# Two delta heads' keys and queries: written by GpSimd straight into the delta rule's tiles, instead of through DRAM

## The chip, the cores and the metric

One core of one Trainium2 chip. The core has five engines that run side by side, each with its own queue of instructions in a fixed order: TensorE (PE in the profile; its weight loads are PEld), VectorE (DVE), ScalarE (ACT), GpSimd (POOL) and SyncE (SP). SP computes nothing here; it issues nearly all the transfers (DMAs) between DRAM and the on-chip memory SBUF. PE writes only into PSUM, the accumulation memory, of which this kernel uses eight banks of 128 x 512 float32. The metric is device microseconds (us) for one execution, the median of several runs.

## The reference

One decoder layer on 1024 tokens of width 1024. A normalised input goes through one projection of 4104 columns. Eight heads of stick-breaking attention and four heads of a gated delta rule work on parts of it, and both results go through an output projection, with a residual and a final norm. For the change only the delta rule's entrance matters:

```python
qkv = jax.nn.silu(causal_depthwise_conv(jnp.concatenate([g_q, g_k, g_v], axis=-1), gdn_conv_w[layer]))
gq, gk, gv = jnp.split(qkv, 3, axis=-1)
gq = l2norm(to_heads(gq, GDN_HEADS, GDN_HEAD_DIM)).astype(x.dtype)
gk = l2norm(to_heads(gk, GDN_HEADS, GDN_HEAD_DIM)).astype(x.dtype)
...
o_gdn = gated_delta_chunked(gq, gk, gv, decay, beta)
```

Here `silu(y)` is `y * sigmoid(y)`: the last product of the projection of a delta head. `gated_delta_chunked` walks the tokens in chunks; each chunk's output needs the state that the chunk before has left.

## The kernel before

The kernel is written with several generators ("streams"): `projections` (the filler, with weight 100 at the end of the file), the delta rule in five streams (`delta_pre`, `delta_load`, `delta_substitute`, `delta_solve`, `delta_scan`), `attention` and `attention_values`, and the output stage. `interleave` takes a step of the most urgent stream that is ready and, where none is, a piece of the filler. "Ready" is judged by `Model`, a planner in the Python code that runs while the program is built: it holds an estimated cost for each instruction and a clock for each engine. The order in which the planner starts instructions on VectorE, ScalarE, GpSimd and SyncE, and in which steps are taken for TensorE, becomes the fixed order of each engine's queue. So an instruction that the planner thinks ready earlier moves in every queue, and so does much of what comes after it. On the chip an engine works strictly down its queue; one whose next instruction is not ready waits.

The filler goes through `ORDER`: projections of the delta heads 0 to 3 (`G0` to `G3`, three kinds each, in the order keys 1, queries 0, values 2), of attention values (`v1`), attention keys (`k0` to `k3`) and gates (`z`). Each kind is two halves of 512 tokens, and each half 24 products of 128x512 (three per 128 rows of the input, since float32 operands are split into a high and a low part). Over the kernel that makes 1152 such products, in the profile `pp<-xh,weh` and the like. The output of one half is handled by `g_evac`: ScalarE copies it out (`pre`), VectorE runs the four taps of the convolution into `ac`, ScalarE takes the sigmoid (over the no longer needed `pre`), and GpSimd multiplies the two (`ac<-ac,pre`).

A unit of the delta rule is half of a head (h, g), 512 tokens in four chunks. Its keys and queries stand in one tile `kq` (128 partitions x 4 chunks x 2 kinds x 128 tokens; `kqf` in the profile, `kwf` where it is read by a transpose), for which SBUF has four fixed slots (`Fixed`, tag "kq"). Before the first delta head these slots hold four rows of the raw input. `delta_load` fetches `kq` with two DMAs from a DRAM copy, `g_s`, that `g_evac` has stored. For the first two heads (`TURNED` = 2) nothing else of the keys is stored, and `gdn_pre` turns keys and queries with eight PE transposes of 128x128; heads 2 and 3 take turned copies from DRAM (`gt_s`). `gdn_pre` then forms the products of each chunk's keys with keys and queries (`pz<-kqf`, 128x256, four a unit), and later multiplies the queries by a decay in place (`kqf<-kqf,cb` on GpSimd). `gdn_chain` is the sequential part; at its end the slot is free for the unit four further on. The values of a delta head (`vt`) come from DRAM in all cases.

Attention values are split and stored (`v_s`) early, and each attention head loads its own into one tile, `v2a`, once the head before has read it.

Nearly all DMAs stand in SP's queue, in the planner's order. All instructions recorded by the planner carry line 363 in the profile (`ins = f(*args, **kw).ins`), so the rows are told apart by their tiles.

Of the kernel before, what the change touches and what calls it, by code (L numbers as in the profile page):

```python
# [10 lines left out]
F32 = mybir.dt.float32  # L11
# [3 lines left out]
ALU = mybir.AluOpType  # L15
AX = mybir.AxisListType

P = 128
# [13 lines left out]
TURNED = 2  # L32
# [4 lines left out]
OUT_WEIGHTS, DELTA, WEIGHTS, BANK, WINDOW, OUTPUT, RESULT, DECAYS = -1, 0, 2, 5, 10, 12, 20, 25  # L37
# [441 lines left out]
def block(tc, xT_d, x_d, n1_d, wE_d, wQ_d, wC_d, conv_d, alog_d, dtb_d, mixw_d, wo_d, fnw_d, out_d):  # L479
    nc = tc.nc  # L480
    ck = Model({"V": nc.vector, "A": nc.scalar, "G": nc.gpsimd, "P": nc.tensor, "S": nc.sync})
    V, A, G, TE, S = ck.V, ck.A, ck.G, ck.P, ck.S

    with ExitStack() as top:
# [7 lines left out]
        fx = Fixed(ck, nc, {**{f"sg{w}": (2048 * (w + 1), 1) for w in range(4)}, "o2": (1024, 1), "kq": (4096, 4), "ak": (4096, 4)})  # L492
# [23 lines left out]
        half = cst.tile([P, SBH], F32, name="half")  # L516
# [18 lines left out]
        g_s = dr.tile([GH, 3, P, T], F32, name="g_s")  # L535
# [21 lines left out]
        def turned(tp, parts):  # L557
            ck.hold(tp)
            for u, a in enumerate(parts):
                if a.dtype == F32R:  # L560
                    TE.transpose(tp[:, u * P:(u + 1) * P].bitcast(F32R), a, idr)
                else:
                    TE.transpose(tp[:, u * P:(u + 1) * P], a, ident)
            ck.free(tp)
            yield from ()
# [58 lines left out]
        for tag, bufs in (("kh", 1), ("kl", 1), ("q2", 1), ("v2a", 1), ("sg2", 1), ("cc", 2), ("cc", 2), ("sg3", 1)):  # L624
            if tag[0] == "s":
                chl.append(fx.tile([P, 2, 520], F32R, "chl", tag))
            else:
                t = at_.tile([P, 1040 + (48 if tag == "kl" else 0)], F32R, tag=tag, bufs=bufs, name="chl")
# [15 lines left out]
        raw, loads = [], {}  # L644
# [78 lines left out]
        def first(f, *args, bank=BANK, **kw):  # L723
            ck.prio, prio = bank, ck.prio
            f(*args, **kw)
            ck.prio = prio
# [49 lines left out]
        flags = {}  # L776
# [88 lines left out]
        def z_evac(i):  # L865
# [9 lines left out]

            return evac

        def g_evac(h, kind):
            wv = conv[:, 4 * kind + h, :]
            last = []  # L880

            def evac(pt, half):
                pre = gd.tile([P, 515], F32, tag="pre", bufs=2, name="pre")
                if half == 0:
                    V.memset(pre[:, 0:3], 0.0)
                else:
                    A.activation(pre[:, 0:3], last[0][:, 512:515], AF.Copy)
                last.append(pre)
                first(A.activation, pre[:, 3:515], pt, AF.Copy)
                ac = pr.tile([P, 512], F32, tag="kt", bufs=2, name="ac")  # L890

                first(A.activation, pt, pre[:, 0:512], AF.Copy, scale=wv[:, 0:1])
                for i in range(1, 4):
                    first(V.scalar_tensor_tensor, ac if i == 3 else pt, pre[:, i:i + 512], wv[:, i:i + 1], pt, ALU.mult, ALU.add)
                sg = pre[:, 0:512]
                first(A.activation, sg, ac, AF.Sigmoid)
                first(G.tensor_tensor, ac, ac, sg, ALU.mult)
                ts = slice(half * 512, half * 512 + 512)
                if h < TURNED:
                    return S.dma_start(g_s[h, kind, :, ts], ac)  # L900
                done = [S.dma_start(g_s[h, kind, :, ts], ac)] if kind < 2 else []
                first(V.transpose, sg, ac)
                turned = gt_s[h, kind, ts, :].rearrange("(b r) d -> r b d", r=32)
                return done + [S.dma_start(turned[:, :, 32 * a:32 * a + 32], sg[32 * a:32 * a + 32, :].rearrange("r (b c) -> r b c", c=32)) for a in range(4)]

            return evac

        def projections():
# [29 lines left out]
            while nxt:  # L938
# [7 lines left out]
                for half in range(2):  # L946
                    hs = slice(half * 512, (half + 1) * 512)
                    wide = name[:2] == "G0" and half
                    yield lambda: ps.room("pz", 4) if wide else ps.room("pp", 2)
                    pt = pz() if wide else pp()  # L950
                    for k in range(NK):
                        n = 8 * half + k
                        if n == 2:
                            nxt = take()
                        if n == 8:
                            split(nxt, 1)
                        if n == 12:
                            split(nxt, 2)
                        h, l = cols.hl[k // 4]
                        mm3(pt, h[:, k % 4, :], l[:, k % 4, :], xh[:, k, hs], xl[:, k, hs], k == 0, k == NK - 1)  # L960
                        if ((k % 4 == 3 if name[0] in 'Gz' else k % 2) or name in ('z0', 'z1', 'z2', 'z3')) and k < NK - 1:
                            yield
                    if half == 0:
                        if name[0] == "G":
                            ev = g_evac(int(name[1]), int(name[2]))
                        else:
                            ev = {"k": k_evac, "z": z_evac}[name[0]](int(name[1]))
                    flags[name if half else name + ".0"] = ev(pt, half)
                    yield
# [21 lines left out]
        def delta_load():  # L991
            yield lambda: "dec" in flags
            for h in range(GH):
                for g in range(2):
                    u = 2 * h + g
                    gst[h, g] = {}
                    half = "" if g else ".0"
                    yield lambda: u < 4 or f"c{u - 4}" in flags
                    if u > 3:
                        yield flags[f"c{u - 4}"]  # L1000
                    kq = fx.tile([P, 4, 2, P], F32, "kq", "kq")
                    ts = slice(512 * g, 512 * g + 512)
                    loads = []
                    for kind in (1, 0):
                        yield lambda: f"G{h}{kind}{half}" in flags
                        loads.append(S.dma_start(kq[:, :, 1 - kind, :], g_s[h, kind, :, ts].rearrange("p (c t) -> p c t", c=4)))
                    ak = fx.tile([P, 2, 4, P], F32, "ak", "ak")
                    kn, at = ak[:, 0], ak[:, 1]
                    nkv = gd.tile([P, 4, P], F32, tag="nkv", bufs=4, name="nkv")
                    gst[h, g].update(kq=kq, kn=kn, nkv=nkv, at=at)  # L1010
                    ck.hold(kq, kn, nkv)
                    turned = lambda kind: gt_s[h, kind, ts, :].rearrange("(c t) d -> t c d", t=P)
                    if h >= TURNED:
                        loads += [S.dma_start(kn, turned(1)), S.dma_start(nkv, turned(0))]
                    flags[f"l{u}g"] = loads
                    yield lambda: f"G{h}2{half}" in flags and (u == 0 or f"q{u - 1}" in flags)
                    vt = gd.tile([P, 4, P], F32 if h >= TURNED else F32R, tag="vt", name="vt")
                    flags[f"v{u}g"] = S.dma_start(vt, turned(2)) if h >= TURNED else S.dma_start(vt.rearrange("p c t -> p (c t)").bitcast(F32), g_s[h, 2, :, ts])
                    gst[h, g].update(vt=vt)
# [566 lines left out]
        def products_attention():  # L1586
            yield lambda: f"d{NB - 1}" in flags
            for b in range(NB):
# [3 lines left out]
                for got in product(b, 0, parts):  # L1592
# [44 lines left out]
        interleave(ck, lambda: ps.room("pz", 4),  # L1637
                   [Stream(delta_scan(), 0, DELTA), Stream(delta_solve(), 0.5, DELTA + 0.5), Stream(delta_substitute(), 0.6, DELTA + 0.6),
                    pre, Stream(delta_load(), 0.4, DELTA + 0.4), Stream(attention(), 9.995, WINDOW), Stream(attention_values(), 9.99, WINDOW), Stream(out_rows(), 9.1, OUT_WEIGHTS), Stream(out_weights(), 9, OUT_WEIGHTS), Stream(out_weights_attention(), 9.25, OUTPUT + 1), Stream(out_rest(), 9.26, OUTPUT + 1), Stream(enter_x(), 9.31, OUTPUT - 4), Stream(out_norm(0), 9.15, OUTPUT - 1), Stream(out_norm(1), 9.16, OUTPUT - 1), fill,
                    Stream(enter_delta(), 9.3, OUTPUT), Stream(prepare(1), 9.2, OUTPUT), Stream(products_delta(), 101, OUTPUT),  # L1640
                    Stream(enter_attention(), 9.1, OUTPUT - 3), Stream(prepare(0), 9.05, OUTPUT - 2), Stream(products_attention(), 102, OUTPUT - 1.5)])
# [38 lines left out]
```

## Time and profile before

| | us |
|---|---|
| median of 3 runs | 637.29 |
| lowest, highest | 636.22, 638.86 |
| the profiled execution | 639.53 |
| its span, first to last instruction | 637.8 |
| PE busy in it | 624.0 |
| granted PE clock, mean | 0.994 |

A row of the profile's tables of groups reads: line, engine, operation, tile written <- tiles read, shapes, xcount, then busy us and mean ns, then the idle time of the engine just before and what ended it. "SPq" is the time that SP takes to issue a transfer, not the transfer. In a timeline a row begins with its start and its duration in us.

### The profile page before, as it was taken

What the parts mean: (1) busy time and instruction counts of PE and PEld (TensorE: products, weight loads), DVE (VectorE), ACT (ScalarE), POOL (GpSimd) and SP (SyncE); (2) the same over time, 40 slices, a digit from 0 to 9 for tenths busy, and PEclk for the clock granted to TensorE, in tenths of its full rate; (3) what the DMA queues carried; (4) which work ended last, traced back from release to release, by engine and by line L of the source; (5) the groups of instructions that cost most, each with busy time, mean ns of one, the idle gap of its engine ahead of it and who ended that gap; (6) DMA issues with size and microseconds to landing.
All of it is one profiled execution on the core that took longest, in us unless ns stands there. A gap on an engine that the chain in (4) does not pass through costs nothing.

```text
span 637.8 us, 11259 instructions
## 1 busy us (share of the span) xinstructions
PE 624.0 (98%) x3672; PEld 528.7 (83%) x3672; DVE 447.5 (70%) x810; ACT 393.9 (62%) x945; POOL 341.2 (53%) x429
## 2 busy tenths in 40 slices
PE   8999999999999999999999989999999999999995
PEld 7889988988888888788888777888888888888884
DVE  4379973322797798887797696777889774478754
ACT  6665567724786776775785866666777653232553
POOL 0124047728794696881679684386764325245522
PEclk9999999999999999999999999899999999999998
DMA  8958337856557466598668768453652578984322
GB/s 305 342 183 312 124 131 253 303 189 222 159 151 224 131 185 134 141 207 221 167 146 224 185 133 264 121 185 94 180 141 84 151 201 255 311 319 143 116 100 100
DMA packets 165563, 120.21 MB, mean 188 GB/s; under 512 B 96448, under 2 KB 131456, under 8 KB 165504
## 3 DMA queue, kind: packets, MB, share of 16 engines
q1 hardware_dynamic: 165216, 119.29, 62.3%
q8 instruction: 29, 0.48, 0.3%
q14 instruction: 30, 0.25, 0.1%
q10 hardware_dynamic: 288, 0.20, 0.1%
HBM read 80.22 MB, written 39.23 MB: 187 GB/s over the span
## 4 chain that ended last, share of the span: by engine, by line
PE 81%; DMA 6%; ACT 4%; DVE 3%; SPq 2%; issue 2%; POOL 1%; POOLq 0%; DVEq 0%; ACTq 0%
PE pp L363 52%; PE pz L363 21%; PE po L363 6%; PE pc L363 3%; SPq L363 2%; DVE cc L363 1%; DMA v2a<-v_s 1%; DMA kh<-qk_s 1%; DMA xr1f<-xT 1%; DMA o_s<-oe 1%; ACT sgf L363 1%; POOL ac L363 1%; DMA qk_s<-sqh 1%; ACT pz L363 1%; DMA cb<-cum_s 1%
## 5 line engine op out<-in xcount | busy, mean ns | idle before, releaser
L363 PE MATMUL pp<-xh,weh 128*128 128x512 f32 x360 | 146.4, 407 | 0.4 <-DVE ac L363 0.4
L363 PE MATMUL pp<-xh,wel 128*128 128x512 f32 x360 | 141.8, 394 | 0.0
L363 PE MATMUL pp<-xl,weh 128*128 128x512 f32 x360 | 141.3, 392 | 0.0
L363 POOL TENSOR_TENSOR sgf<-sgf,cc 128x128 f32<-128x128 f32 (+3 forms) x64 | 77.5, 1216 | 57.7 <-DVE cc L363 52.5
L363 POOL TENSOR_TENSOR wel<-wer,weh 128x512 fp32r<-128x512 f32 x48 | 62.5, 1305 | 72.0 <-ACT weh L363 71.6
L363 PEld LDWEIGHTS pp<-xh,wel 128*128 128x128 f32 x360 | 68.0, 189 | 15.3
L363 PEld LDWEIGHTS pp<-xh,weh 128*128 128x128 f32 x360 | 68.1, 189 | 12.8 <-DVE ac L363 0.9
L363 PEld LDWEIGHTS pp<-xl,weh 128*128 128x128 f32 x360 | 68.1, 189 | 11.5
L363 DVE TENSOR_TENSOR_SCAN cc<-pz,step 128x384 f32<-128x384 f32 (+2 forms) x64 | 53.4, 844 | 10.6 <-ACT pz L363 9.5
L363 ACT ACTIVATE sgf<-pz,rs 128x384 f32<-128x384 f32 (+3 forms) x96 | 53.5, 593 | 7.6 <-PE pz L363 7.6
L363 DVE TENSOR_TENSOR ahl<-pz,ahl 128x512 fp32r<-128x512 f32 (+1 forms) x80 | 49.5, 630 | 12.0 <-ACT ahl L363 11.3
L363 ACT ACTIVATE ahl<-pz 128x512 fp32r<-128x512 f32 (+1 forms) x80 | 43.2, 559 | 20.6 <-PE pz L363 20.1
L363 ACT ACTIVATE pz<-pz,ns 128x384 f32<-128x384 f32 (+3 forms) x96 | 52.5, 576 | 0.0
L363 PE MATMUL po<-ahl,v2a 128*128 128x512 f32 (+1 forms) x160 | 48.9, 400 | 2.4 <-DMA v2a<-v_s 2.3
L363 PE MATMUL pp<-wo,mmf 128*128 128x512 f32 x192 | 45.5, 396 | 0.0
L363 DVE SCALAR_TENSOR_TENSOR pp<-pre,conv,pp 128x512 f32<-128x512 f32 x42 | 31.4, 747 | 18.2 <-ACT pp L363 17.8
L363 PEld LDWEIGHTS pp<-wo,mmf 128*128 128x128 f32 x192 | 35.8, 188 | 8.4
L363 PE MATMUL pp<-woh,mmf 128*128 128x512 f32 (+2 forms) x136 | 41.9, 385 | 0.0
L363 DVE TENSOR_TENSOR_SCAN cc<-pz,cc,step 128x512 f32<-128x512 f32 (+1 forms) x32 | 38.8, 1211 | 4.1 <-ACT pz L363 3.0
L363 POOL TENSOR_TENSOR mmf<-mgf,mmf 128x512 fp32r<-128x512 f32 x16 | 21.9, 1366 | 37.0 <-ACT mmf L363 23.9
L363 POOL TENSOR_TENSOR ac<-ac,pre 128x512 f32<-128x512 f32 x24 | 31.0, 1293 | 16.3 <-ACT pre L363 10.9
L363 DVE TENSOR_TENSOR xr<-pp,xr 128x512 f32<-128x512 f32 (+2 forms) x33 | 22.2, 672 | 23.0 <-PE pp L363 23.0
(317 smaller groups left out, 1513.9 us busy)
## 6 DMA issues: line engine op xcount, KB each, us to landing
wer<-wE SPq DMA_DIRECT2D x48, 256.0 KB, 3.5
xr<-x SPq DMA_DIRECT2D x16, 512.0 KB, 7.6
g_s<-ac SPq DMA_DIRECT2D x20, 256.0 KB, 2.3
v_s<-v2e SPq DMA_DIRECT2D x16, 256.0 KB, 3.3
kqf<-g_s SPq DMA_DIRECT2D x16, 256.0 KB, 4.0
v2a<-v_s SPq DMA_DIRECT2D x8, 512.0 KB, 5.9
q<-qk_s SPq DMA_DIRECT2D x8, 512.0 KB, 4.5
kh<-qk_s SPq DMA_DIRECT2D x8, 512.0 KB, 3.9
```

The lines of the kernel that those rows point to most:

```text
L363: ins = f(*args, **kw).ins
```

## The change

For the keys and queries of heads 0 and 1, GpSimd's last product goes directly into the unit's `kq` tile, chunk by chunk, instead of over `ac`; the store to `g_s` and the load from it go. The tile is taken from its slot when the first such product is recorded (`operand`), no longer when the load is due. `delta_load` hands on the product itself as the thing to wait for. Values of all heads, and everything of heads 2 and 3, stay as they were.

```diff
+        operands = {}
+
+        def operand(h, g):
+            if (h, g) not in operands:
+                operands[h, g] = fx.tile([P, 4, 2, P], F32, "kq", "kq")
+                ck.hold(operands[h, g])
+            return operands[h, g]
...
                 first(A.activation, sg, ac, AF.Sigmoid)
+                ts = slice(half * 512, half * 512 + 512)
+                if h < TURNED and kind < 2:
+                    kq = operand(h, half)
+                    ck.prio, prio = BANK, ck.prio
+                    r = G.tensor_tensor(kq[:, :, 1 - kind, :], ac.rearrange("p (c t) -> p c t", c=4), sg.rearrange("p (c t) -> p c t", c=4), ALU.mult)
+                    ck.prio = prio
+                    return r
                 first(G.tensor_tensor, ac, ac, sg, ALU.mult)
-                ts = slice(half * 512, half * 512 + 512)
                 if h < TURNED:
                     return S.dma_start(g_s[h, kind, :, ts], ac)
...
-                    kq = fx.tile([P, 4, 2, P], F32, "kq", "kq")
+                    kq = operand(h, g)
                     ts = slice(512 * g, 512 * g + 512)
                     loads = []
                     for kind in (1, 0):
                         yield lambda: f"G{h}{kind}{half}" in flags
-                        loads.append(S.dma_start(kq[:, :, 1 - kind, :], g_s[h, kind, :, ts].rearrange("p (c t) -> p c t", c=4)))
+                        loads.append(flags[f"G{h}{kind}{half}"] if h < TURNED else S.dma_start(kq[:, :, 1 - kind, :], g_s[h, kind, :, ts].rearrange("p (c t) -> p c t", c=4)))
...
-                    ck.hold(kq, kn, nkv)
+                    ck.hold(kn, nkv)
```

On PE, at the end of head 0's projection (the difference of the two orders; `pp` and `pz` are banks, `step` holds the identity matrix for the transposes, `chl` the weights of the attention values):

```order
 L363 MATMUL pp<-xl,weh 128x512
 L363 MATMUL pp<-xh,wel 128x512
+L363 MATMUL pz<-step,kwf_1119 128x128 x8
 L363 MATMUL pp<-xh,weh 128x512
 L363 MATMUL pp<-xl,weh 128x512
@@ -465,4 +466,5 @@
 L363 MATMUL pz<-xl,weh 128x512
 L363 MATMUL pz<-xh,wel 128x512
+L363 MATMUL pz<-kqf_889 128x256 x4
 L363 MATMUL pp<-chl,xh 128x256 x2
 L363 MATMUL pp<-chl,xl 128x256
```

The eight transposes of the first unit now stand after the 12th of the 24 products of the first half of head 0's values, and its four products of keys right behind that projection; both used to stand among the attention values' products further down. On GpSimd the instructions ahead of the first unit's two products are the same as before.

On SP, in the same stretch (`dtf`, `dt`, `cb` and `cum_s` belong to the decays of all heads, `wer` are weights):

```order
-L363 DMA g_s<-ac 128x512 x2
-L363 DMA kqf_1074<-g_s 128x4x128
 L363 DMA cum_s<-cs 32x2x128
-L363 DMA dtf_1009<-cum_s 128x512
-L363 DMA g_s<-ac 128x512
-L363 DMA dtf_1017<-cum_s 128x512
+L363 DMA dtf_1008<-cum_s 128x512
+L363 DMA dtf_1016<-cum_s 128x512
 L363 DMA dt<-cum_s 128x512
```

The stores and loads of keys and queries are gone, and the decay loads stand next to each other. In the whole program SP has 16 transfers fewer, eight `g_s<-ac` and eight `kqf<-g_s`.

Much further on, on SP, ahead of the load of attention head 3's values (`o_s` are attention outputs, `gt_s` turned delta operands, `bd` and `br` belong to the delta rule's inverse). Before:

```order
L363 DMA o_s<-oe 32x8x32 x4
L363 DMA cb<-cum_s 128x512
L363 DMA dt<-dt_s 128x512
L363 DMA wer<-wE 128x512 x2
L363 DMA g_s<-ac 128x512
L363 DMA gt_s<-pre 32x16x32 x4
L363 DMA v2a<-v_s 128x8x128
```

And now:

```order
L363 DMA o_s<-oe 32x8x32 x3
L363 DMA br<-bd 64x1x496 x2
L363 DMA wer<-wE 128x512 x2
L363 DMA o_s<-oe 32x8x32
L363 DMA g_s<-ac 128x512
L363 DMA gt_s<-pre 32x16x32 x4
L363 DMA v2a<-v_s 128x8x128
```

The decay loads `cb` and `dt` of a delta unit no longer stand ahead of this load. Between the last product that reads one attention head's `v2a` and the first that reads the next head's, PE's order had 60 projection products for head 3 and 30 for head 4; it now has 36 and 42. The last head's last such product stands after 1056 of the 1152 projection products before, after 1089 now.

## The prediction, made before the run

> **What bounds the kernel now.** I read the page first, for the busy shares, then the table by stage, then the list of what TensorE (PE) waited for, then the queue of SP, from which nearly every transfer is issued.
>
> ```profile
> span 637.8 us, 11259 instructions
> PE 624.0 (98%) x3672; PEld 528.7 (83%) x3672; DVE 447.5 (70%) x810; ACT 393.9 (62%) x945; POOL 341.2 (53%) x429
> PE 81%; DMA 6%; ACT 4%; DVE 3%; SPq 2%; issue 2%; POOL 1%; POOLq 0%; DVEq 0%; ACTq 0%
> ```
>
> PE is busy for 624.0 of 637.8 us, and 81% of the chain that ended last is PE. So the kernel ends when PE has worked off a list that is fixed at build time; another engine, or a transfer, matters only where PE reaches an instruction too early. About 13.8 us of the span have no PE work. The table by stage (columns: PE, weight loads, DVE, ACT, POOL, then granted clock and DMA) says where:
>
> ```profile
> 0.00:16.00 16.00, 14.20 (x58) 11.70 (x59) 7.26 (x16) 9.74 (x14) 0.98 (x7) 1.00 0.85 306
> ...
> 112.00:128.00 16.00, 15.71 (x129) 15.30 (x128) 5.08 (x14) 12.59 (x41) 11.55 (x16) 1.00 0.88 311
> ...
> 352.00:368.00 16.00, 14.18 (x76) 11.33 (x74) 11.13 (x20) 15.19 (x54) 10.68 (x15) 1.00 0.75 198
> 368.00:384.00 16.00, 15.04 (x76) 12.63 (x77) 15.20 (x25) 9.41 (x19) 12.83 (x11) 1.00 0.60 132
> 384.00:400.00 16.00, 14.50 (x153) 12.05 (x152) 9.65 (x21) 10.26 (x34) 6.90 (x12) 0.96 0.90 267
> 400.00:416.00 16.00, 16.00 (x88) 13.16 (x87) 11.45 (x22) 9.93 (x24) 6.92 (x7) 0.94 0.43 120
> ...
> 624.00:640.00 16.00, 7.21 (x42) 6.25 (x40) 5.42 (x12) 3.99 (x11) 3.99 (x6) 0.82 0.25 99
> ```
>
> The first slice lacks 1.80 us (loading) and the last slice 6.6 of the 13.8 us that belong to the span (the tail after the last product). Neither is touched. Between them PE lacks 13.8 - 1.8 - 6.6 = 5.4 us, of which the three slices from 352 to 400 us hold 1.82 + 0.96 + 1.50 = 4.3. The eight slices from 80 to 208, in which heads 0 and 1 enter the delta rule, add up to 127.71 of 128 us of PE work (below), and all of their 0.29 us lies between 112 and 128. The clock column adds a second loss: (1 - 0.96) and (1 - 0.94) of 16 us make 1.6 us lost to a lower clock between 384 and 416. Which wait ends last there:
>
> ```profile
> PE po L363 <- DMA v2a<-v_s: 2.3, 1, 2.3
> PE po L363 <- DVE step L363: 1.7, 1, 1.7
> PE pz L363 <- ACT wy L363: 1.5, 1, 1.5
> PE pz L363 <- DVE cc L363: 0.6, 2, 0.4
> PE pp L363 <- DVE ac L363: 0.4, 1, 0.4
> PE pz L363 <- ACT nkv L363: 0.3, 1, 0.3
> ```
>
> ```profile
> sum 128.00, PE 127.71 PEld 110.22 DVE 71.48 ACT 82.41 POOL 84.70; mean PE 15.96 PEld 13.78 DVE 8.94 ACT 10.30 POOL 10.59
> ```
>
> Neither the spill `g_s` nor the key and query tile `kq` (called `kqf` in the trace) is in this list. The largest named wait is one load of attention values, `v2a`.
>
> **The change, part by part.** First the product itself.
>
> ```profile
> L363 POOL TENSOR_TENSOR ac<-ac,pre 128x512 f32<-128x512 f32 x24 | 31.0, 1293 | 16.3 <-ACT pre L363 10.9 <-issue 4.5 <-POOL wy L363 0.8
> L363 POOL TENSOR_TENSOR kqf<-kqf,cb 128x512 f32<-128x512 f32 x8 | 10.3, 1287 | 6.6 <-PE pz L363 6.6
> ```
>
> Eight of the 24 products on POOL now write into `kq`, whose rows of 128 lie 256 elements apart. The second row is a product that already reads and writes exactly that layout: 1287 ns against 1293. The eight cost 8 x (1287 - 1293) ns, which is nothing.
>
> Second, the transfers. Eight stores and eight loads of 256 KB go.
>
> ```profile
> g_s<-ac SPq DMA_DIRECT2D x20, 256.0 KB, 2.3
> kqf<-g_s SPq DMA_DIRECT2D x16, 256.0 KB, 4.0
> L363 SPq DMA_DIRECT2D g_s<-ac x20: 319/330/751, 88.7 to 339.8; - x20
> L363 SPq DMA_DIRECT2D kqf<-g_s x16: 371/434/522, 91.2 to 380.6; - x16
> 182.60 0.38 SPq L363 DMA_DIRECT2D kqf<-g_s  x1
> q1 hardware_dynamic: 165216, 119.29, 62.3%
> ```
>
> On SP's queue that is 8 x 0.33 + 8 x 0.43 = 6.1 us of issue time, all of it before 185 us (the last `kqf` load of head 1 goes out at 182.6), and 4.2 of 119.29 MB. For a unit (half a head) the operand is there one store, one issue and one load earlier, 2.3 + 0.4 + 4.0 = 6.7 us. What stood behind those sixteen on SP (the decay loads `dtf`, the weights `wer`, `cb`, `vt`) moves up. On PE it is worth next to nothing now: the delta steps of heads 0 and 1 lie among projection products, and the whole stretch of 80 to 208 us lacks 0.29 us, which the `ACT nkv` row names at 0.3. In the new order the eight transposes and their squares come ahead of the values' projection, so I count that row as gone: **-0.3 us**. If the cover went (a transpose reached before POOL's product was done) PE would wait; the product that it needs ended in time before:
>
> ```profile
> 96.42 1.29 POOL L363 TENSOR_TENSOR ac<-ac,pre 128x512 f32<-128x512 f32 x1 [1.90 <-ACT pre L363]
> 95.62 5.44 PE pp L363 x24
> ```
>
> This is the third product, head 0's queries, first half. It ends at 97.71. The new place of the transposes is after 12 of the 24 products that begin at 95.62, at about 95.62 + 12 x 0.227 = 98.3 (5.44 / 24 = 0.227). Some 0.6 us of margin: the bounds of this wait are 0 and about one POOL instruction, 1.3 us, if another slips in front. I take 0, since the instructions ahead of it on POOL stay the same. Nothing else on PE can be late there but the projection behind it.
>
> Third, **what the new order moves elsewhere**. The planner sees the delta rule ready earlier and lays out everything behind it anew, on all engines. PE's instructions are the same ones, so the sum of the work is unchanged, and only the waits can differ. The one I can follow is `v2a`: each head's load goes out after the head before has read the tile, from an SP queue that is late.
>
> ```profile
> 303.27 1.06 PE L363 MATMUL po<-ahl,v2a 128*128 128x512 f32 x4
> 305.12 0.45 SPq L363 DMA_DIRECT2D cb<-cum_s  x1
> 305.61 1.98 SPq L363 DMA_DIRECT2D dt<-dt_s  x1
> 310.75 1.59 SPq L363 DMA_DIRECT2D wer<-wE  x2
> 314.77 2.04 SPq L363 DMA_DIRECT2D gt_s<-pre  x4
> 316.91 0.48 SPq L363 DMA_DIRECT2D v2a<-v_s  x1
> 324.76 0.59 PE L363 MATMUL po<-ahl,v2a 128*128 128x512 f32 x2
> 350.97 1.06 PE L363 MATMUL po<-ahl,v2a 128*128 128x512 f32 x4
> 361.87 0.38 SPq L363 DMA_DIRECT2D v2a<-v_s  x1
> 361.87 7.05 DMA v2a<-v_s
> 368.96 0.62 PE L363 MATMUL po<-ahl,v2a 128*128 128x512 f32 x2 [2.33 <-DMA v2a<-v_s]
> ```
>
> Head 3: last read over at 304.3, issue at 316.9, 12.6 us late, behind weights and the transposed stores; first use 7.85 us after the issue, so 0.8 us to spare against the 7.05 of the other load. Head 4: read over at 352.0, issue 9.8 us late, and PE waits 2.33. In the new order PE has 36 projection products between the two uses of head 3 where it had 60, and 42 where it had 30 for head 4. At 0.227 us that is 5.4 us less cover for head 3 and 2.7 us more for head 4. With SP as late as before, head 4's 2.3 us vanish and head 3 waits 5.4 - 0.8 = 4.6: together +2.3. With head 3's load early enough, only the -2.3 stays. SP's rows ahead of head 3's load are about as many as before, but `cb` and `dt` (305.12 to 307.6 on SP) are no longer among them; those two were followed by a wait for `wer` that would have hidden their going. So the bounds are -2.3 and +2.3. I take **-1.0**, nearer to the lower end, because the planner puts the first use where it expects the tile to have landed, and in six of seven heads of the trace PE did not wait there.
>
> Sum: 0 - 0.3 - 1.0 = -1.3 us. The profiled execution took 639.53 us (span 637.8, the rest around it), 2.2 above the median of 637.29; it becomes 638.2, and the median **636.0**. A difference of 0.5%, 3.2 us, is about what a measurement of this kernel can tell from no change; so the forecast is "no change that can be told", on the fast side.
>
> The lower clock is a place to weigh a rule. The two rows lost 1.6 us though PE was busy for 14.50 of 16 us and never waited longer than 2.3 us at once. The Trainium skill, "TensorE: Matmul & The Clock Gate", section "Part 1: The HAM clock gate (the "warmup" mystery)", says that the clock falls to half after an idle window of about 3.4 us. By it no fall would be due here; the trace shows one, so the measurement decides.
>
> **The rivals.**
>
> *Middle waits go (faster).* The waits from 352 to 400 us are coincidences of one order, and the new one may not have them: -4.3 - 0.3 gives 632.7. For it: with less on SP, the tightest stretch starts differently. Against: SP is relieved only up to 185 us, a stretch in which PE lacks 0.29 us. With every middle wait and the clock's 1.6 gone the end is -5.4 - 1.6 = -7.0, that is 630.3.
>
> *Head 3's values come late (slower).* Same mechanism as above, other end: 36 products cover too little of 12.6 + 7.05 us, and head 4's wait is not won back since its load again stands behind a row of SP's that waits. +4.6 for head 3 gives 641.9. It decides from an issue more than 12.6 - 4.6 = 8.0 us behind the last read. For it: the attention stream as a whole now stands later against the projections (PE ends its last head's values after 1089 of 1152 products, before after 1056), so cover at the end shrinks as well. Against: the rows ahead of the load are no more than before.
>
> *Nothing reaches PE.* The waits are redone at the same size, 637.3. For it: PE's list is the same, and no wait named `kqf` or `g_s`.
>
> *A second fall of the clock.* A new wait among the many small products of the delta rule's inverse costs another 1.6 us: 636.0 + 1.6 = 637.6. By the skill's window it would take an idle PE of 3.4 us first.
>
> **How the numbers follow.** Forecast 0.42, middle waits gone 0.25, head 3 late 0.21, nothing 0.06, second fall 0.06. Faster by over 0.5% means below 634.1, slower above 640.5. Faster: nearly all of the 0.25 and 0.04 of the forecast's spread, 0.28. Slower: 0.19 of the 0.21 and 0.01 of the clock's, 0.20. The rest, 0.52, is no change. The range takes in both rivals' prices, 632.7 and 641.9, with 1 us beyond the lower one towards its bound of 630.3: 631.5 to 642.0.
>
> **What would show it.** Right: eight products `kqf<-ac` of about 1.29 us on POOL; 12 stores `g_s` and 8 loads `kqf` left; the first transposes of `kq` at about 98 us (not 109.9 as now) with no PE wait for POOL; head 4's wait for `v2a` gone and head 3's below 2 us. Wrong: a POOL product well over 1.3 us, a PE wait on `kqf` near 98 us, head 3 waiting 4 us or more, or a new wait for a transfer in the middle, which would mean that the order's side effects outweigh the transfers that went. An end outside the range would show that the rest of the order, which I did not follow, decides.

## The result, and the profile after

| | before | after |
|---|---|---|
| median | 638.08 us (4 runs) | 647.17 us (4 runs) |
| lowest, highest | 636.22, 640.95 | 646.23, 647.54 |
| ratio, 95% interval | | 1.0149 (1.0123 to 1.0174) |
| profiled execution, its span | 639.53, 637.8 | 647.01, 645.3 |

The changed kernel is slower by 1.5%, 9.1 us, and lies outside the range of 631.5 to 642.0. (The ratios here and below are those of the undisturbed runs, and need not be the quotient of two medians.) The page of the changed kernel, with the lines that were shown of before:

```profile
span 645.3 us, 11215 instructions
PE 626.1 (97%) x3672; PEld 530.1 (82%) x3672; DVE 452.6 (70%) x810; ACT 394.0 (61%) x945; POOL 343.1 (53%) x429
PE 76%; DMA 6%; POOL 5%; DVE 4%; issue 4%; ACT 2%; SPq 2%; POOLq 0%; DVEq 0%; ACTq 0%
```

The span grew by 7.5 us; nearly all of the rest of the 9.1 is that the profiled execution of before lay 1.5 us above its median. PE works off the same 3672 products; its busy time grew by 626.1 - 624.0 = 2.1, and the time without PE work from 13.8 to 645.3 - 626.1 = 19.2, by 5.4. The table by stage (columns as before; the last three are granted clock, DMA share, GB/s) says where:

```profile
256.00:272.00 16.00, 12.44 (x59) 10.32 (x58) 9.40 (x18) 9.27 (x33) 9.46 (x9) 0.89 0.81 195
272.00:288.00 16.00, 14.91 (x74) 12.05 (x73) 14.40 (x27) 13.71 (x34) 13.15 (x19) 1.00 0.60 147
...
352.00:368.00 16.00, 15.65 (x88) 12.98 (x87) 10.99 (x20) 13.12 (x49) 6.09 (x7) 1.00 0.76 185
368.00:384.00 16.00, 13.26 (x48) 10.54 (x49) 9.46 (x15) 6.20 (x17) 12.80 (x16) 0.79 0.95 237
384.00:400.00 16.00, 16.00 (x149) 13.13 (x148) 11.48 (x24) 12.89 (x41) 9.05 (x14) 1.00 0.59 160
...
576.00:592.00 16.00, 14.46 (x70) 11.66 (x70) 12.59 (x18) 3.46 (x5) 6.66 (x4) 1.00 0.29 95
```

Two of these slices as they were before:

```profile
256.00:272.00 16.00, 15.60 (x79) 12.78 (x79) 13.34 (x24) 12.75 (x43) 13.48 (x10) 1.00 0.61 134
...
576.00:592.00 16.00, 16.00 (x78) 12.97 (x77) 12.94 (x20) 4.12 (x9) 6.52 (x5) 1.00 0.40 125
```

In the stretch from 352 to 400 us, PE lacks 0.35 + 2.74 = 3.1 us where it lacked 4.3; its waits of before are gone, and the 2.74 is a new one. Also new are 3.56 + 1.09 us from 256 to 288 and 1.54 from 576 to 592 (before: 0.40 and none). The granted clock is low in two of these slices, 0.89 and 0.79, which by the column makes 1.8 + 3.4 = 5.1 us; before had 0.96 and 0.94 in two later slices, 1.6 us. The list of what PE waited for:

```profile
PE pz L363 <- DVE cc L363: 4.9, 3, 3.6
PE pp L363 <- POOL wel L363: 2.7, 1, 2.7
PE po L363 <- DVE step L363: 1.7, 1, 1.7
PE pp L363 <- ACT mmf L363: 1.5, 1, 1.5
PE pp L363 <- DVE zt L363: 0.5, 1, 0.5
PE pp L363 <- DVE v2e L363: 0.4, 1, 0.4
```

Neither `v2a` nor `nkv` nor `kqf` is in it. The row of `step` (1.7) is the one of before, at the kernel's start; of the others `cc` was at 0.6 before and the rest absent. The first of the new waits, at 260 us, in the timeline of the changed kernel, on SP, DVE and PE (start, us, engine, operation, tile, count, in brackets the idle time before and its end):

```profile
254.44 2.10 SPq L363 DMA_DIRECT2D xs<-xd  x1
256.65 1.00 SPq L363 DMA_DIRECT2D wer<-wE  x2
258.01 1.59 SPq L363 DMA_DIRECT2D gt_s<-pre  x3
257.55 0.65 DVE L363 TENSOR_TENSOR_SCAN cc<-pz,step 128x256 f32<-128x256 f32 x1
262.14 0.06 DVE L363 MEMSET pre<- 128x3 f32 x1 [3.93 <-DMA gt_s<-pre]
262.20 2.07 DVE L363 TENSOR_TENSOR_SCAN cc<-pz,step 128x384 f32<-128x384 f32 x2
263.30 0.43 PE L363 MATMUL pz<-step,stf 128*128 128x128 f32 x3 [3.56 <-DVE cc L363]
```

It is read from the bottom. PE waits for an attention scan `cc`. The scan stands on DVE behind a memset of 0.06 us that clears the head of a convolution tile `pre`; the memset waits 3.93 us until the stores that read this tile have landed. Those stores stand on SP behind `xs<-xd`, which holds SP for 2.10 us. Three queues, each in a fixed order, pass one late row on to an attention step that has nothing to do with it. The second wait, at 375 us, on ACT, POOL and PE:

```profile
368.95 0.67 ACT L363 ACTIVATE weh<-wer 128x512 fp32r<-128x512 f32 x1
369.43 1.55 POOL L363 TENSOR_TENSOR tt<-yx,xb 128x512 f32<-128x512 f32 x1
373.26 1.04 POOL L363 TENSOR_TENSOR norms<-norms,half 128x4 f32<-128x4 f32 x1
374.43 1.46 POOL L363 TENSOR_TENSOR qn<-ss,root 128x4 f32<-128x4 f32 x1
376.65 1.26 POOL L363 TENSOR_TENSOR wel<-wer,weh 128x512 fp32r<-128x512 f32 x1
377.97 0.79 PE L363 MATMUL pp<-xh,wel 128*128 128x512 f32 x1 [2.74 <-POOL wel L363]
```

The weights' high part is ready at 369.6; their low part `wel`, which needs only that, stands on POOL behind the delta rule's inverse and its norms, and starts 7 us later.

### The profile page after: what moved, and what is told of

Read it like the earlier page. It is cut to its first block, busy times and chain, and to the rows that moved or that the text cites. A ratio compares the mean times of both kernels' runs of the same rounds, so it can differ in the third digit from the quotient of the medians.

```text
span 645.3 us, 11215 instructions
## 1 busy us (share of the span) xinstructions
PE 626.1 (97%) x3672; PEld 530.1 (82%) x3672; DVE 452.6 (70%) x810; ACT 394.0 (61%) x945; POOL 343.1 (53%) x429
## 4 chain that ended last, share of the span: by engine, by line
PE 76%; DMA 6%; POOL 5%; DVE 4%; issue 4%; ACT 2%; SPq 2%; POOLq 0%; DVEq 0%; ACTq 0%
PE pp L363 44%; PE pz L363 22%; PE po L363 6%; PE pc L363 3%; SPq L363 2%; DVE cc L363 1%; POOL mmf L363 1%; DMA gt_s<-pre 1%; DMA worf<-wo 1%; DMA dtf<-cum_s 1%; POOL tt L363 1%; DMA og_s<-akf 1%; POOL oss L363 1%; DVE pp L363 1%; DMA bothf<-o_s 1%
## 5 line engine op out<-in xcount | busy, mean ns | idle before, releaser
L363 PEld LDWEIGHTS pz<-step,stf 128*128 128x128 f32 x288 | 30.7, 141 | 8.3 <-issue 3.7
L363 PE MATMUL pz<-step,stf 128*128 128x128 f32 x288 | 34.0, 244 | 3.6 <-DVE cc L363 3.6
```

## The experiments

The theory to start from: the direct write itself costs nothing; the order that the planner lays out for it does, through rows like the two above. The rival: the write, or the lack of the transfers, costs by itself.

### The cross: the write without its order, and the order without the write

The first kernel has the direct write in the order of before. The planner still records the old product, stores and loads, and rows without an instruction are left out at the end:

```diff
+        def ghost(out, src):
+            op = ck.record("S", None, [out], [src], cost("S", "dma_start", (out, src), {}), None)
+            op.port = False
+            return op
...
+                    ins = nc.gpsimd.tensor_tensor(kq[:, :, 1 - kind, :], ac.rearrange("p (c t) -> p c t", c=4), sg.rearrange("p (c t) -> p c t", c=4), ALU.mult).ins
...
+                    op = ck.record("G", ins, [ac], [ac, sg], cost("G", "tensor_tensor", (ac, ac, sg, ALU.mult), {}), None)
...
+                    return ghost(g_s[h, kind, :, ts], ac)
...
-                        loads.append(S.dma_start(kq[:, :, 1 - kind, :], ...))
+                        loads.append((ghost if h < TURNED else S.dma_start)(kq[:, :, 1 - kind, :], g_s[h, kind, :, ts].rearrange("p (c t) -> p c t", c=4)))
...
+                    ck.hold(kq, kn, nkv)
...
         for ops in ck.order.values():
+            ops = [o for o in ops if o.ins is not None]
```

> The eight products of heads 0 and 1 go straight into the delta rule's slots and the sixteen transfers are gone, but every engine keeps the order of before: the planner is told that the stores and loads are still there, and they are left out at the end. Theory (the new order is what costs): 635.5 to 638.5 us, that is 0.996 to 1.001 of before, with waits of PE in the middle as in before (v2a of head 4 about 2.3 us). Rival (the direct write itself costs: the slots held for long, POOL's product into a strided tile, or transfers that used to space out others): 644 to 648 us, ratio 1.010 to 1.016, with the waits at 260 and 375 us of the changed kernel still there.

The second has the order of the changed kernel, with the stores and loads put back on SP: the store 0.2 us after the planner finishes the product, the load 4.5 us behind it. The planner still believes that the product itself fills the tile:

```diff
+                    dst, a3, s3 = kq[:, :, 1 - kind, :], ac.rearrange("p (c t) -> p c t", c=4), sg.rearrange("p (c t) -> p c t", c=4)
+                    ins = nc.gpsimd.tensor_tensor(ac, ac, sg, ALU.mult).ins
+                    r = ck.record("G", ins, [dst], [a3, s3], cost("G", "tensor_tensor", (dst, a3, s3, ALU.mult), {}), None)
...
+                    r.post = [nc.sync.dma_start(g_s[h, kind, :, ts], ac).ins,
+                              nc.sync.dma_start(dst, g_s[h, kind, :, ts].rearrange("p (c t) -> p c t", c=4)).ins]
...
     def finish(self, op):
         op.end = self.now
+        for n, ins in enumerate(getattr(op, "post", ())):
+            self.at(self.now + 200 + 4500 * n, self.put, ins)
```

> The other half of the cross: PE, VectorE, ScalarE and POOL run in the order of the changed kernel, but the eight stores and eight loads of heads 0 and 1 are put back on SP's queue, each at the time at which the planner has the product ready. Theory (the new order costs): 645 to 650 us, ratio 1.011 to 1.02, with the PE waits for the scans at 260 us and for POOL's wel at 375 us as in the changed kernel, perhaps a new wait near 98 us, where the transposes now stand earlier than a load may land. Rival (the direct write costs): 636 to 640 us.

| order | through DRAM | written directly |
|---|---|---|
| of before | 637.42 | 637.59, ratio 1.001 (0.9987 to 1.0034) |
| of the change | 661.14, ratio 1.0367 (1.0334 to 1.04) | 647.17, ratio 1.0149 (1.0123 to 1.0174) |

In the order of before the write changes nothing that can be told; the waits are nearly those of before (the one for `wy`, 1.5 us, is not there), headed by the same one:

```profile
PE po L363 <- DMA v2a<-v_s: 2.8, 1, 2.8
```

In the new order the transfers cost 14 us more, which neither theory had foreseen. The timeline of that kernel (a longer source, so line 368 instead of 363) shows where most of it begins, at the transposes of head 0 and again of head 1, and its list of waits still has the changed kernel's:

```profile
106.38 1.23 PE L368 MATMUL pz<-step,kwf 128*128 128x128 f32 x8 [8.01 <-DMA kqf<-g_s]
187.68 1.23 PE L368 MATMUL pz<-step,kwf 128*128 128x128 f32 x8 [3.84 <-issue]
...
PE pz L368 <- DVE cc L368: 4.5, 3, 2.6
PE pp L368 <- POOL wel L368: 2.5, 1, 2.5
```

The new order puts the transposes where a direct write has the tile ready, and a load has not. So the early start of the delta rule is real, and used; only the order that uses it is slower than the old one even with the write. That the write itself costs nothing is shown in the old order alone; in the new one it cannot be taken out without these two waits.

### Mending the new order row by row

First the stores alone, then `wel` as well, then two products on POOL as well; each is a piece of a queue's list, moved ahead of another row:

```diff
+        move("S", 227, 3, 224, "gt<-pre", "xs<-xd")
+        move("G", 282, 1, 271, "wel<-", "tt<-yx")
+        move("G", 283, 2, 278, "sg", "r2b<-")
```

> The changed kernel with the first of the two edits alone: three stores gt_s<-pre ahead of the xs store on SP's queue. Theory: VectorE's memset of pre no longer waits 3.9 us, PE's 3.56 us at 260 us go, and the clock stays at 1.0 from 256 to 272 us: 647.2 - 3.6 - 1.7 = 641.9 us, between 641 and 643.5; the wait at 375 us stays. Rival (the wait has another cause, such as the PE order or the stores' own time): 645.5 to 648 us.

> The changed kernel with two places of its order mended: on SP's queue three stores of the transposed second head go out ahead of the xs store that waits (254.4 us), and on POOL the second wel of the third inverse comes ahead of the first tt<-yx,xb (371 us). Theory: the wait at 260 us (3.56 us, and about 1.7 us of half clock) and the one at 375 us (2.74 us, and about 3.4 us of half clock) both vanish: 647.2 - 11.4 = 636, and up to 640 if something else is late just behind either. Rival (both waits are symptoms of PE running at its earliest, so that the next wait takes their place; or the clock's falls have another cause): 643 to 648 us.

> The changed kernel with the two edits of after_both and a third: on POOL the two products sgf<-sgf,cc that stood behind the norms of the third inverse (377.9 us) go out ahead of r2b (about 375.5 us), since PE waited 2.29 us for the scans behind them once wel was mended. Theory (each wait is one misplaced row): 643.8 - 2.3, and the stretch of 0.90 clock with it, 640 to 642. Rival (POOL's chain of the inverse is simply full there, so that whatever goes first makes another late): 643 to 645.5.

| rows moved | median | ratio (95%) | span | PE busy | no PE work |
|---|---|---|---|---|---|
| none | 647.17 | 1.0149 (1.0123 to 1.0174) | 645.3 | 626.1 | 19.2 |
| stores | 644.92 | 1.0108 (1.008 to 1.0136) | 642.9 | 623.8 | 19.1 |
| stores, `wel` | 643.77 | 1.0097 (1.0065 to 1.0129) | 642.6 | 624.4 | 18.2 |
| stores, `wel`, `sgf` | 642.62 | 1.0072 (1.0049 to 1.0095) | 642.3 | 624.6 | 17.7 |

Of the three waits, 3.56, 2.74 and 2.29 us, the one for `wel` went and the other two shrank, and in the sum less came back than they held. With the stores mended, PE's wait at 261 us is 0.15 in place of 3.56, but others came up, in that kernel's timeline:

```profile
261.21 0.42 PE L363 MATMUL pz<-step,stf 128*128 128x128 f32 x3 [0.15 <-DVE cc L363]
271.97 0.49 PE L363 MATMUL pz<-state,kqf 128*128 128x128 f32 x2 [1.25 <-ACT pz L363]
...
365.55 0.49 PE L363 MATMUL pc<-xct,xinv 128*128 128x128 f32 x2 [1.01 <-DVE xct L363]
```

The time without PE work is the same to 0.1 us; nearly all of the 2.4 us that the span gained are in PE's busy time. The changed kernel has 3.4 and 6.8 us at half clock in its middle, this one none. With `wel` mended too, its wait is gone and the next one stands 1.5 us behind its place, for a scan whose factor `sgf` waits on POOL behind the same norms:

```profile
377.85 1.91 POOL L363 TENSOR_TENSOR sgf<-sgf,cc 128x384 f32<-128x384 f32 x2
379.49 3.12 PE L363 MATMUL pz<-kqf 128*128 128x256 f32 x8 [2.29 <-DVE cc L363]
```

With all three moved, the two that shrank are 1.15 us (at 261.85) and 1.01 us (at 379.00). The theory of misplaced rows asked for 641 to 643.5, 636 to 640 and 640 to 642 us; all three kernels missed it, the second lay in its rival's range, and the other two between the ranges, nearer to the rival's. Half of the loss, 4.6 of 9.1 us by the medians, came back; of the 5.4 us more without PE work only 1.5. That PE, spared one wait, reaches the next step of the delta rule's or the attention's chain sooner than that is ready fits all three copies; that no further rows would bring back the rest is not shown. The third new wait, 1.54 us at 584 (`mmf`), was not tried.

### The one row that the forecast had followed, moved in the old order

```diff
+        move("S", 386, 1, 374, "v2a<-", "xd")
```

> The kernel before, with its sixteen transfers, and the same one row of SP's queue moved. If the direct write is worth nothing by itself, this kernel gains what direct_v2a gains, within 1 us: 637.4 - 2.3 = 635.1, range 632 to 636.5. If the direct write gives something that the other waits had hidden, direct_v2a is faster than this one by over 1 us.

> The direct write with the order of before (the kernel of the first experiment), and on SP's queue the load of v2a for head 4 goes out ahead of the three gt-inverse loads and weights it stood behind (before xd<-xs at 354 us instead of at 362 us). PE waited 2.76 us for it there, and after the wait the granted clock was 0.79 for 16 us. Theory (one misplaced row costs its wait and sometimes a stretch of half clock): 637.6 - 2.8 = 634.8, with the clock's fall gone too 631.5; range 631 to 636. Rival (the next wait just behind takes its place, as in the mended copies of the changed kernel, which got back 3.4 of 11.4 us): 636 to 638.

Before with this row moved: 637.09 us, ratio 0.9999 (0.9981 to 1.0016). The direct write in the order of before with it: 638.96, ratio 1.0023 (1.0007 to 1.0039). Both lie outside what was expected, 632 to 636.5 and 631 to 636 (for the second, its rival's 636 to 638 too). The wait for `v2a` is gone in both, and no time with it that can be told. In the first kernel's timeline, and its table in slices of 4 us (PE, granted clock, DMA share, GB/s):

```profile
364.79 1.13 PE L363 MATMUL pz<-kqf 128*128 128x256 f32 x4 [0.45 <-DVE cc L363]
369.56 0.45 PE L363 MATMUL pz<-step,stf 128*128 128x128 f32 x3 [1.41 <-DVE cc L363]
...
391.59 0.74 PE L363 MATMUL po<-ahl,v2a 128*128 128x512 f32 x2 [0.21 <-DVE ahl L363]
...
390.00:394.00 4.00, 3.79 (x88) 0.93 0.96 348
394.00:398.00 4.00, 4.00 (x26) 0.50 1.02 251
398.00:402.00 4.00, 4.00 (x22) 0.72 0.96 276
```

Two waits for scans stand where the one for the load stood, 1.86 us of its 2.33, and in this execution the clock takes the rest: by its column 0.3 + 2.0 + 1.1 = 3.4 us are lost here, 1.6 in before. The clock is not what hides a gain in general, though: the executions with a granted clock of 0.996 or more took 636.0 to 637.3 us with the row moved (8 of 12), and 636.0 to 637.8 in before (11 of 23). So the wait of 2.3 us was worth nothing that can be told (the interval leaves a gain of at most 1.2 us), and the direct write gains nothing when it goes. No kernel of this study beats before.

### Is it this order, or any new order?

`SLACK` is the time that the planner adds before it takes an operand of PE as arrived. It changes no work, only the order (with 460 and 600 that takes two loads of activation tables less on ScalarE, 8 in place of 10):

```diff
-SLACK = 450
+SLACK = 460
```

> The kernel before with one constant of the planner changed: SLACK 460 ns in place of 450, with nothing of the work changed, only the order laid out from it. Theory A (the time of this program hangs on which waits an order happens to meet, and a new order costs as such): the order differs in a few hundred rows and the time moves by 1 to 12 us either way, 636 to 650. Theory B (the changed kernel's loss is systematic: a delta rule that the planner believes ready earlier is put in too early): within 2 us of before, 636 to 640.

> The changed kernel with SLACK 460 in place of 450. Theory A (the loss is one order's coincidences): the waits at 260 and 375 us are not the same ones, and the time may lie anywhere from 636 to 650 us. Theory B (the loss is systematic for a delta rule that is ready earlier): 645 to 650 us, with waits of the same kind, for the scans and for wel, at the same places.

> The kernel before with SLACK 600, which lays out nearly all of it anew. Theory A: 638 to 652 us, as far from before as the changed kernel is, though it holds all sixteen transfers. Theory B: within 3 us of before.

> The changed kernel with SLACK 600. Theory A: anywhere from 636 to 652 us, and not the worse of the two with SLACK 600 in particular: the difference of the two lies within 6 us of nothing, with either sign. Theory B: 6 to 12 us above the kernel before with SLACK 600.

> The kernel before with SLACK 300. Theory A (any order laid out anew costs, because each meets its own waits): 639 to 648 us, as SLACK 460 and 600 gave 0.6 and 0.8 per cent more. Theory B (a delta rule that is ready earlier is what costs): within 4 us of before, and clearly below the changed kernel with the same SLACK.

> The changed kernel with SLACK 300. Theory A: within 4 us of the kernel before with SLACK 300, with either sign. Theory B: 4 to 12 us above it.

> The kernel before with SLACK 900. Theory A: 640 to 655 us (PE's operands are awaited with more reserve, so projection products are used up earlier). Theory B: clearly below the changed kernel with the same SLACK.

> The changed kernel with SLACK 900. Theory A: within 4 us of the kernel before with SLACK 900, with either sign. Theory B: 4 to 12 us above it.

| SLACK | through DRAM, ratio (95%) | written directly, ratio (95%) | direct less DRAM |
|---|---|---|---|
| 300 | 1.0179 (1.0157 to 1.0201) | 1.0176 (1.0115 to 1.0236) | -0.0003 |
| 450 | 1 | 1.0149 (1.0123 to 1.0174) | +0.0149 |
| 460 | 1.006 (1.0034 to 1.0086) | 1.0076 (1.0046 to 1.0107) | +0.0016 |
| 600 | 1.0082 (1.005 to 1.0114) | 1.0119 (1.0071 to 1.0168) | +0.0037 |
| 900 | 1.021 (1.0181 to 1.0238) | 1.0274 (1.0246 to 1.0302) | +0.0064 |

All are relative to the kernel before; the direct kernel's ratio at 300 rests on three runs from 644.4 to 651.3 us. Ten nanoseconds more in one constant of the planner make the old kernel 0.6% slower and the changed one 0.7% faster. The orders with 300, 600 and 900 have lists of waits of their own, though the changed kernel with 600 still waits 1.36 us for `wel` at 379 us. Of the old kernel with 600:

```profile
PE pz L363 <- ACT pz L363: 3.2, 2, 2.3
PE pz L363 <- ACT vr L363: 2.6, 1, 2.6
```

With 460 this is not so. The changed kernel's two main waits stand where they stood (263.30 and 377.97 us with 450), as theory B had said and against theory A:

```profile
263.64 0.42 PE L363 MATMUL pz<-step,stf 128*128 128x128 f32 x3 [2.39 <-DVE cc L363]
378.62 0.50 PE L363 MATMUL pp<-xh,wel 128*128 128x512 f32 x1 [2.41 <-POOL wel L363]
```

Its time, 643.2 us, is below the 645 to 650 of theory B all the same, and its old twin keeps the wait for `v2a` (2.7 us at 370) and is at 641.3. The old kernel with 300, at 649.2, lies above what either theory had for it.

At three of the four other values the pair's intervals overlap; the mean difference of the four is 0.3%, a fifth of that at 450. A loss of 4 to 12 us each time, as theory B had it, did not come: by the ratios it is -0.2, 1.0 and 2.4 us at 300, 460 and 600. At 900 it is 4.1, where alone the intervals are apart, and there theory B's range holds. By the medians the direct kernel is the slower at all four, by 1.9 to 4.2 us. So a systematic loss of 2 to 4 us may stand behind the 9.1; these runs do not settle it. The order of before is the fastest of all ten; whether 450 was once picked for that, the record does not say.

## Why the prediction was wrong, step by step

- **The product and the transfers: right.** On POOL, among the transfers, and at 97 us the signs are as named:

```profile
L363 POOL TENSOR_TENSOR kqf<-ac,pre 128x512 f32<-128x512 f32 x8 | 10.3, 1290 | 7.2 <-ACT pre L363 7.1
g_s<-ac SPq DMA_DIRECT2D x12, 256.0 KB, 2.7
kqf<-g_s SPq DMA_DIRECT2D x8, 256.0 KB, 3.3
95.33 1.29 POOL L363 TENSOR_TENSOR kqf<-ac,pre 128x512 f32<-128x512 f32 x1 [1.84 <-ACT pre L363]
97.14 0.79 PE L363 MATMUL pz<-step,kwf 128*128 128x128 f32 x8
```

  Eight products of 1290 ns, no PE wait at the transposes, 0.5 us of margin (estimated: 0.6). By itself, in the order of before, the write is worth nothing (1.001).
- **The `nkv` row, -0.3: gone, but not gained.** PE now waits 0.4 us for `v2e` at 114 us, in the same slice: from 112 to 128 it is busy for 15.60 us, before for 15.71.
- **`v2a`: right in its signs, wrong in its price.** Head 4's wait went and head 3 did not get one, so the rival "head 3's values come late" fell. But the step counted the wait as its 2.3 us. The kernel with that row moved alone gained nothing that can be told, and two scans stood just behind it. The rival "middle waits go" priced the waits from 352 to 400 us in the same way, as if nothing came in their place.
- **What the new order moves elsewhere, -1.0 with bounds of -2.3 and +2.3: the step that failed.** It followed one tile and took that tile's bounds for the whole order's. In place of -1.0 us the span grew by 7.5: 5.4 us more without PE work, through rows that the forecast did not follow (the stores ahead of 260 us, `wel` at 375, `mmf` at 584), and 2.1 us more in which PE is busy, though "the sum of the work is unchanged". The cross puts the +1.5% on this step, since the write in the old order is at 1.001. Its width could have been measured: four more orders of the old kernel cost 0.6 to 2.1%, while the stated range reached from -0.9 to +0.7%. The argument that "the planner puts the first use where it expects the tile to have landed" speaks for any order alike, and these runs show what it is worth.
- **The clock: a further fall was named, its place and size were not met.** The rival expected a new wait among the small products of the delta rule's inverse and 1.6 us. Instead the clock fell with the waits for the attention scan (264.7 us) and for `wel` (377.3 us); by its column that is 5.1 us against 1.6 in before, and PE's busy time grew by 2.1.
- The last sentence of the forecast, that an end outside the range would mean that the rest of the order decides, is what the cross shows. The named sign "a new wait for a transfer in the middle" appeared at 260 us, by way of DVE.

## What to carry to other kernels

In a program whose order is laid out by a planner, an edit that frees an operand earlier is two changes: the edit, and a new order of everything behind it. Measure them apart, by the edit in the old order and by the old program in a few other orders; the spread of the latter is the width that a forecast needs. In these runs a wait that went was worth no more than the way to the next late thing, so the rows of a list of waits are not to be added up.

## What the hardware did that was not expected

The granted clock does not follow the length of PE's waits. In the changed kernel it fell to half 0.7 us before PE came out of a wait of 2.74 us; with the stores mended, a wait of 2.84 us at the same instruction left it at 1.00 (table by stage of each, PE, clock, DMA share, GB/s):

```profile
264.00:265.00 1.00, 1.00 (x6) 0.83 0.95 300
...
377.00:378.00 1.00, 0.03 (x1) 0.65 1.04 383
378.00:379.00 1.00, 1.00 (x3) 0.50 0.92 252
```

```profile
378.44 0.50 PE L363 MATMUL pp<-xh,wel 128*128 128x512 f32 x1 [2.84 <-POOL wel L363]
...
368.00:384.00 16.00, 12.93 (x63) 1.00 0.91 228
```

What counts is how a wait lies in time. By the clock column in slices of 1 us, all nineteen stretches at half clock in the seventeen traces, the kernels' ends left out, last 3.4, 6.8 or 10.2 us, and the falls within one trace lie whole multiples of 3.413 us apart: the changed kernel's, at 264.66 and 377.30 (the rows with 0.83 and 0.65), 33 multiples; those of the old kernel with SLACK 300, at 277.06 and 399.94, 36. So the clock is set in steps of 3.41 us, on a grid that does not begin anew with a wait:

| kernel | step of its grid, us | without PE work in it | clock after it |
|---|---|---|---|
| changed | 261.26 to 264.67 | 2.04 | half |
| changed | 373.90 to 377.31 | 2.08 | half |
| stores mended (grid from the fall at its end, 640.18) | 373.94 to 377.35 | 1.74 | full |
| the same | 377.35 to 380.77 | 1.10 | full |
| before, `v2a` row moved | 390.03 to 393.44 | 0.21 | half |

In these traces each step at full clock with over 1.85 us without PE work ended in a fall, and of those with 1.4 to 1.85 us some did. The last row of the table stands alone: the clock fell at 393.44 us with no PE wait of over 0.21 us in the 20 us ahead (the row at 391.59 above). Some 2.0 us of that step were products of 32x32; whether that is the reason these runs do not show. The Trainium skill, "TensorE: Matmul & The Clock Gate", section "Part 1: The HAM clock gate (the "warmup" mystery)", has the clock at half after an idle window of about 3.4 us; the traces here show falls after steps of that length of which about 2 us were idle, and one after 0.21 us.

A power of 128x4 elements on POOL (`norms<-norms,half`, `qn<-ss,root`) took 1.04 and 1.46 us, nearly as long as a product of 128x512 (1.26 to 1.55); a product of 128x4 (`r2b<-r2b,beta`) took 0.20.
